# A two-layer trunk on one core: sums of weight blocks built in DRAM ahead of time, a seven-tile ring for weights, splits put forward

## The chip, the core and the metric

The kernel runs on one core of a Trainium2 chip, as one launch. The metric is the device time of that launch in microseconds (us): 1351.71 us is the median of 3 runs of the kernel before. Engines are named as in the profile: PE multiplies matrices, DVE and ACT work on tiles, POOL (GpSimd) does some tile work and issues transfers, SP issues transfers only.

## The reference, cut to what matters

The input is 512 positions of width 1024. Two layers follow, each a mixer (layer 0: gated delta net, layer 1: stick-breaking attention, both beside a small memory attention), an output projection, and an MLP of hidden width 4096. Only the lines that matter here:

```python
for i in range(DEPTH):                      # DEPTH = 2
    h = rms_norm(x, norm_pre_mix[i])
    proj = h @ (w_in_a if i == 0 else w_in_b)[0]
    ...
    x = x + rms_norm(y, norm_post_mix[i])
    h = rms_norm(x, norm_pre_mlp[i])
    y = jnp.square(jax.nn.relu(h @ w_up[i])) @ w_down[i]
    x = x + rms_norm(y, norm_post_mlp[i])
```

Everything is float32.

## The kernel before, in words

**Products.** A float32 product is done as three products of rounded parts: each operand is split into a high and a low part, and PE does high·high, high·low and low·high (`mm3`). A weight block of 512 KB (a piece) is loaded by SP into one of three tiles named `raw` (`raw`, L172). ACT copies it to the high part `whi` (L182) and DVE subtracts to get the low part `wlo` (L163); there are four places for such pairs. So a piece that is loaded early waits in `raw`, and the split waits for a free pair.

**Stages.** The span has, in order: the start and the memory keys (to about 50 us), the delta net of layer 0 (50 to 340), its output projection, the MLP of layer 0 (about 388 to 720), the attention of layer 1 (720 to 950), its output projection, the MLP of layer 1 (1005 to the end).

**The delta net.** `w_in_a` comes in 27 pieces, one for each call of `fm_slices`, which yields three times within a piece; `weave` puts the pieces' products between the steps of the recurrence. POOL does small work for the recurrence here, in its program order: masks (`dr_hi`, `dr_lo`, L382 and L383; `Dm`, L392), clears of `Q` (L489), and once for each group of heads the sum `vb` (L565), which PE transposes next (L368).

**The MLP.** The up product fills 32 chunks of hidden activations, 16, then 12, then 4. The down product of the 16 and of the 12 uses a scheme of seven products for each 2 by 2 block (`mlp_down`), with 4 and 3 blocks in the two groups, so 28 and 21 products in a layer. Its seven steps multiply combinations of the activations with combinations of four weight quarters B(0,0), B(0,1), B(1,0), B(1,1) of 512 KB each. `weave` puts the up pieces of the next group between them. The last 4 chunks go through `mlp_last` in the plain way.

**How the weight combinations are made before.** For each block, step 1 loads B(0,0) by SP into one of four tiles `xc` (`load`, L860). Steps 2, 3 and 7 add another quarter to that same tile by a transfer of POOL that accumulates (`plus`, L864). Step 4 loads B(0,0) again into `raw` and lets DVE subtract it from `xc` (`less`, L869). Steps 5 and 6 load a quarter plainly. In each step DVE also forms the activations' combination (`comb`, `minus`), ACT and DVE split it into `sh` (L902 and L163), and at the end of a step its result goes into `mixT` (L918).

**Order.** Each engine executes its own list in order. The list is the order of the code, changed by priorities: the scheduler may let an instruction that is ready go ahead of earlier code. `keep_in_program_order` ties an instruction to the one written before it on its engine and does not tie what comes after.

Of the kernel before, what the change touches and what calls it, by code (L numbers as in the profile page):

```python
# [8 lines left out]
F32 = mybir.dt.float32  # L9
# [4 lines left out]
ALU = mybir.AluOpType  # L14
# [15 lines left out]
MAGIC = float(0x5F3759DF)  # L30
NUA, NX, NSH = 15, 4, 4
NRAW = 3
NDM = 2
# [25 lines left out]
def drain(gen):  # L59
    for _ in gen:  # L60
        pass


class Trunk:
    def __init__(self, ctx, tc, a, out):
        self.ctx, self.tc, self.nc, self.a, self.out = ctx, tc, tc.nc, a, out
        pool = lambda **k: ctx.enter_context(tc.tile_pool(**k))
        self.const = pool(name="const", bufs=1)
        self.wp = pool(name="wp", bufs=1)
        self.act = pool(name="act", bufs=1)  # L70
        self.small = pool(name="small", bufs=3)
        self.ps = pool(name="ps", bufs=4, space=PSUM)
        self.decays = {}
        self.constants()
# [95 lines left out]
    def raw(self, src):  # L170
        raw = self.wp.tile(list(src.shape), F32, name="raw", tag="raw", bufs=NRAW)
        self.nc.sync.dma_start(out=raw, in_=src)  # L172
        return raw

    def halves(self, raw, alloc=None):
        shape = list(raw.shape)
        if alloc:
            hi, lo = alloc(F32R, shape), alloc(F32R, shape)
        else:
            hi = self.wp.tile(shape, F32R, name="whi", tag="whi", bufs=NW)  # L180
            lo = self.wp.tile(shape, F32R, name="wlo", tag="wlo", bufs=NW)
        self.nc.scalar.activation(out=hi, in_=raw, func=AF.Copy)  # L182
        self.split_lo(lo, raw, hi)
        return hi, lo
# [18 lines left out]
    def fm_slices(self, src, hi, lo, done, tag="acc"):  # L203
# [3 lines left out]
        for k0, k1 in ((0, 3), (3, 6), (6, 8)):  # L207
            self.fm_part(b, piece, hi, lo, k0, k1)
            if k1 == KC:
                done(b)  # L210
            yield (k1 - k0) * 3 * MM

# [621 lines left out]
    def mlp_up(self, i, c0, n, hi, lo, done):  # L834
# [4 lines left out]
        for c in range(c, c0 + n):  # L839
            yield from self.fm_slices(self.a["w_up"][i, c], hi, lo, done)  # L840

    def mlp_down(self, i, c0, nd, us, yacc, first, tail=None):

# [3 lines left out]
        nc, v = self.nc, self.nc.vector  # L847
        wd = self.a["w_down"][i]
        A, X = [], [None] * nd
        for d in range(nd):  # L850
# [3 lines left out]
        def B(d, kh, j):  # L854
            r0 = (c0 + 2 * (kh * nd + d)) * P
            return wd[r0:r0 + 2 * P, j * 512:(j + 1) * 512].rearrange("(z p) n -> p z n", p=P)

        def load(d):
            X[d] = self.ring("xc")
            nc.sync.dma_start(out=X[d], in_=B(d, 0, 0))  # L860
            return X[d]

        def plus(d, x, kh, j):
            nc.gpsimd.dma_start(out=x, in_=B(d, kh, j), accum_op=ALU.add)  # L864
            return x

        def less(d):
            x = self.raw(B(d, 0, 0))
            v.tensor_tensor(out=x, in0=X[d], in1=x, op=ALU.subtract)  # L869
            return x  # L870

# [4 lines left out]
        def minus(d):  # L876
# [4 lines left out]

        steps = (
            ("b", True, lambda d: A[d][11], lambda d: load(d), ((0, 0, 1),)),
            ("c", True, lambda d: comb(d, 21, 21, ALU.subtract, 22), lambda d: plus(d, X[d], 0, 1), ((1, 1, 1),)),
            ("b", False, lambda d: comb(d, 21, 21, ALU.subtract, 11), lambda d: plus(d, X[d], 1, 1), ((0, 1, -1),)),
            ("b", False, minus, lambda d: less(d), ((1, 1, -1),)),
            ("c", False, lambda d: comb(d, 21, 12, ALU.add, 21), lambda d: self.raw(B(d, 1, 1)), ((0, 1, 1),)),
            ("c", True, lambda d: A[d][12], lambda d: self.raw(B(d, 1, 0)), ((0, 0, 1),)),
            ("b", False, lambda d: A[d][22], lambda d: plus(d, X[d], 1, 0), ((1, 0, 1),)),
        )  # L890
        regions = {n: [self.bank("g") for _ in range(2)] for n in "bc"}
        fresh = {(r, j): first for r in range(2) for j in range(2)}
        for n, (name, new, left, right, outs) in enumerate(steps):
# [3 lines left out]
            for d in range(nd):  # L897
                w = right(d)
                whi, wlo = self.halves(w)
                src = left(d)  # L900
# [52 lines left out]

    def mlp(self, i, hi, lo, done):
        yacc = self.act.tile([P, NT, D], F32, name="mixT", bufs=1)
        groups = [{"n": 0, "t": []} for _ in GROUPS]
# [9 lines left out]
        for g, us in enumerate(groups):  # L966
# [5 lines left out]
            c += GROUPS[g]  # L972
        drain(tail)


# [126 lines left out]
def build(ctx, tc, a, out):  # L1102
# [14 lines left out]
    with tc.tile_pool(name="start", bufs=1) as sp:  # L1117
# [4 lines left out]
        for t in range(NT):  # L1122
# [3 lines left out]
            if t % 2:  # L1126
                k.to_T(t // 2, xs[t - 1:], k.g_pre[0], hi, lo)
        drain(kv)
    with tc.tile_pool(name="gdn", bufs=1, reuse_waits="tile") as gp:
        k.gdn_constants(gp)  # L1130
# [30 lines left out]
        for gi in range(3):  # L1161
            weave(k.gdn_group(gi, parts[gi], gp, mixT), fill(gi), SCALE[gi])
    keep = [dram.tile([P, D], F32, name=f"keep{t}") for t in range(NT)]

# [13 lines left out]
    with tc.tile_pool(name="mlp0", bufs=1, reuse_waits="tile") as k.mlpp:  # L1178
# [10 lines left out]
        k.mlp(0, hi, lo, done)  # L1189
        hi, lo = hi2, lo2  # L1190
    with tc.tile_pool(name="sb", bufs=1, reuse_waits="tile") as sp:
        tc.keep_in_program_order(nc.scalar.preload_act_table_set("natural_log_exp_and_others"))
# [39 lines left out]
    with tc.tile_pool(name="mlp1", bufs=1, reuse_waits="tile") as k.mlpp:  # L1232
# [6 lines left out]
        hi, lo = k.h_tiles()  # L1239
        k.out_proj(1, mixT, st, parked(1, k.next_norm(k.g_mlp[1], hi, lo)))  # L1240
        k.mlp(1, hi, lo, store)

# [55 lines left out]
```

## Time and profile before

| | |
|---|---|
| Median of 3 runs | 1351.71 us (1351.01 to 1354.47) |
| The profiled execution | 1353.73 us, of which the span is 1352.0 us |
| PE busy | 1290.3 us (95%) |
| DVE, ACT, POOL busy | 874.3, 723.8, 168.3 us |
| Mean busy share of the 16 transfer engines | queue of SP 26.5%, queue of POOL 12.9% |

A row of a time line reads: start, duration, engine, line, operation, out<-in, count, and in brackets the idle time before it and what ended that. A row of the windows gives the busy time of each engine in a stretch, its granted clock (PEclk, 1.00 is full), the mean busy share of the 16 transfer engines and GB/s.

### The profile page before, as it was taken

To read this page: it belongs to the slowest core of one execution; us is meant where nothing else is said; L and a number is where in the kernel's file an instruction comes from. 1 tells how busy PE (TensorE), PEld (TensorE's weight loads), DVE (VectorE), ACT (ScalarE), POOL (GpSimd) and SP (SyncE) were. 2 spreads that over 40 slices of the span, in tenths; PEclk is the share of its full clock that TensorE was granted. 3 is DMA by queue.
4 is the path that set the end of the run, shared out by engine and by line. 5 is a ranking of instruction groups with operands and counts; after the bars stand their busy time and mean duration, and the time that the engine had idled before them with its cause. 6 is when DMAs were issued, how large, how long until landed. Compare 5 with 4: busy or idle time off the path is not lost.

```text
span 1352.0 us, 18018 instructions
## 1 busy us (share of the span) xinstructions
PE 1290.3 (95%) x6620; PEld 1075.6 (80%) x6620; DVE 874.3 (65%) x1650; ACT 723.8 (54%) x1426; POOL 168.3 (12%) x194
## 2 busy tenths in 40 slices
PE   7999999998999999999989999988999999998987
PEld 6788888786798888887768987776798888887866
DVE  7677695876752366556678678889663356554866
ACT  8654535445554454454456577778555445444542
POOL 2511202000000111002000012223000021002100
PEclk9899999989999999999999999999999999999989
DMA  6421121112543465547644311110553365654732
GB/s 235 141 84 57 48 63 48 48 48 78 188 156 97 91 139 131 172 125 130 160 140 141 110 63 48 48 47 32 187 172 109 94 119 123 180 150 100 169 112 78
DMA packets 58409, 150.66 MB, mean 111 GB/s; under 512 B 4928, under 2 KB 10048, under 8 KB 58320
## 3 DMA queue, kind: packets, MB, share of 16 engines
q1 hardware_dynamic: 42256, 112.74, 26.5%
q0 software_dynamic: 15488, 35.72, 12.9%
q8 instruction: 52, 0.85, 0.3%
q10 hardware_dynamic: 576, 1.05, 0.2%
q14 instruction: 37, 0.30, 0.1%
HBM read 140.57 MB, written 8.91 MB: 111 GB/s over the span
## 4 chain that ended last, share of the span: by engine, by line
PE 58%; DVE 6%; ACT 4%; issue 2%; DMA 1%; POOL 0%; DVEq 0%; ACTq 0%; POOLq 0%
PE ps_acc L195 33%; PE ps_g L909 20%; PE ps_g L195 2%; PE ps_g L1057 1%; DMA raw<-w_down 1%; DVE wlo L163 1%; DMA xc<-w_down 1%; PE ps_g L277 1%; PE ps_acc L1074 1%; POOL sb_al L1063 0%; ACT scrap L263 0%; DVE ua L163 0%; ACT whi L182 0%; ACT sb_e L1038 0%; DVE sbkk L163 0%
## 5 line engine op out<-in xcount | busy, mean ns | idle before, releaser
L195 PE MATMUL ps_acc<-h_hi,wlo 128*128 128x512 f32 (+1 forms) x888 | 337.3, 380 | 3.7 <-DVE wlo L163 3.7
L195 PE MATMUL ps_acc<-h_hi,whi 128*128 128x512 f32 (+1 forms) x888 | 339.7, 382 | 1.2 <-DVE sbkk L163 1.2
L195 PE MATMUL ps_acc<-h_lo,whi 128*128 128x512 f32 (+1 forms) x888 | 336.0, 378 | 0.0
L163 DVE TENSOR_TENSOR wlo<-raw,whi 128x1024 fp32r<-128x1024 f32 x167 | 209.8, 1258 | 187.6 <-ACT whi L182 179.5
L182 ACT ACTIVATE whi<-raw 128x1024 fp32r<-128x1024 f32 x167 | 176.9, 1060 | 253.1 <-PE ps_acc L195 126.8
L909 PE MATMUL ps_g<-whi,sh 128*128 128x512 f32 x784 | 259.6, 396 | 3.6 <-DVE sh L163 2.5
L195 PEld LDWEIGHTS ps_acc<-h_hi,wlo 128*128 128x128 f32 x888 | 168.0, 189 | 34.8 <-DVE wlo L163 4.6
L195 PEld LDWEIGHTS ps_acc<-h_hi,whi 128*128 128x128 f32 x888 | 168.5, 190 | 29.7 <-DVE sbkk L163 1.5
L195 PEld LDWEIGHTS ps_acc<-h_lo,whi 128*128 128x128 f32 x888 | 168.5, 190 | 28.3
L909 PEld LDWEIGHTS ps_g<-whi,sh 128*128 128x128 f32 x784 | 147.3, 188 | 40.4 <-DVE sh L163 3.4
L909 PE MATMUL ps_g<-wlo,sh 128*128 128x512 f32 x392 | 155.2, 396 | 0.7 <-DVE wlo L163 0.7
L163 DVE TENSOR_TENSOR wlo<-xc,whi 128x1024 fp32r<-128x1024 f32 x56 | 67.9, 1222 | 68.5 <-ACT whi L182 67.9
L864 POOL DMA_DIRECT2D xc<-w_down x42 | 50.2, 1199 | 485.8 <-DVE wlo L163 409.8
L182 ACT ACTIVATE whi<-xc 128x1024 fp32r<-128x1024 f32 x56 | 59.0, 1057 | 96.2 <-PE ps_g L909 72.9
L909 PEld LDWEIGHTS ps_g<-wlo,sh 128*128 128x128 f32 x392 | 73.9, 189 | 18.7 <-DVE wlo L163 1.9
L163 DVE TENSOR_TENSOR sh<-ua,sh 128x512 fp32r<-128x512 f32 x98 | 66.8, 685 | 9.5 <-ACT sh L902 9.5
L195 PE MATMUL ps_acc<-ua 128*128 128x512 f32 x224 | 63.3, 415 | 8.0 <-ACT ua L182 7.4
L1063 POOL TENSOR_TENSOR sb_al<-sb_a,sb_ah 128x128 fp32r<-128x128 f32 (+3 forms) x48 | 46.7, 973 | 163.3 <-DVE sb_ah L1062 130.0
L902 ACT ACTIVATE sh<-ua 128x512 fp32r<-128x512 f32 x98 | 60.7, 619 | 10.7 <-DVE ua L163 10.4
L195 PEld LDWEIGHTS ps_acc<-ua 128*128 128x128 f32 x224 | 43.8, 200 | 20.1 <-ACT ua L182 8.3
L869 DVE TENSOR_TENSOR raw<-xc,raw 128x1024 f32<-128x1024 f32 x14 | 17.1, 1223 | 44.4 <-DMA raw<-w_down 27.1
L195 PE MATMUL ps_acc<-whi,h_hi 128*128 128x256 f32 (+1 forms) x144 | 44.6, 328 | 0.0
(351 smaller groups left out, 2154.0 us busy)
## 6 DMA issues: line engine op xcount, KB each, us to landing
raw<-w_up SPq DMA_DIRECT2D x64, 512.0 KB, 3.8
raw<-w_down SPq DMA_DIRECT2D x50, 512.0 KB, 4.4
xc<-w_down POOLq DMA_DIRECT2D x42, 512.0 KB, 6.4
raw<-w_in_a SPq DMA_DIRECT2D x27, 512.0 KB, 3.6
raw<-w_out SPq DMA_DIRECT2D x16, 512.0 KB, 3.6
xc<-w_down SPq DMA_DIRECT2D x14, 512.0 KB, 3.9
raw<-w_b_qk SPq DMA_DIRECT2D x14, 512.0 KB, 3.7
park<-xc POOLq DMA_DIRECT2D x8, 512.0 KB, 3.3
```

The lines of the kernel that those rows point to most:

```text
L163: self.nc.vector.tensor_tensor(out=lo, in0=src, in1=f(hi), op=ALU.subtract)
L182: self.nc.scalar.activation(out=hi, in_=raw, func=AF.Copy)
L195: self.nc.tensor.matmul(out, lhsT=l, rhs=r, start=start and k == 0 and i == 0, stop=stop and k == n - 1 and i == 2)
L277: nc.tensor.transpose(b[:, j, i * P:(i + 1) * P], xs[i][:, (kc + j) * P:(kc + j + 1) * P], self.ident)
L864: nc.gpsimd.dma_start(out=x, in_=B(d, kh, j), accum_op=ALU.add)
L869: v.tensor_tensor(out=x, in0=X[d], in1=x, op=ALU.subtract)
L902: nc.scalar.activation(out=s[:, 0], in_=src, func=AF.Copy)
L909: nc.tensor.matmul(y[t], lhsT=l, rhs=r, start=new and d == 0 and z == 0 and m == 0, stop=d == nd - 1 and z == 1 and m == 2, skip_group_che ...
L1057: nc.tensor.matmul(zb[:, off:n], lhsT=l, rhs=x, start=False, stop=m == len(ops) - 1, skip_group_check=True)
L1063: nc.gpsimd.tensor_tensor(out=u["al"], in0=a, in1=f(u["ah"]), op=ALU.subtract)
L1074: nc.tensor.matmul(ob[:, i * P:], lhsT=v, rhs=r, start=i == NT - 1 and m == 0, stop=i == 0 and m == 1, skip_group_check=True)
```

## The change

1. `prepare(i)` makes four DRAM tiles for each of the seven blocks of layer i: the sums 1 (B(0,0)+B(0,1)), 2 (sum 1 + B(1,1)), 3 (B(0,1) alone, then + B(1,1)) and 4 (sum 2 + B(1,0)), with the signs of the scheme left to the activations. It queues 56 operations: 28 copies from DRAM to DRAM on SP's queue and 28 accumulating transfers into DRAM on POOL's queue, in the waves copy 1, copy 3, plus 1, plus 3, copy 2, plus 2, copy 4, plus 4, seven of each. Each is tied to program order on its engine.
2. The queue is emptied from `fm_slices`, `rate` operations when a piece's last matmuls are written: 3 for each piece of the delta net (layer 0's sums), 1 for each piece in the MLP of layer 0, 2 in the attention of layer 1 (layer 1's sums).
3. In `mlp_down` the seven weight blocks are plain loads: three of quarters, four of sums. The 21 accumulations, 7 loads into `xc` and 7 DVE subtractions of a layer are gone.
4. Inside `mlp` the four `xc` tiles join the three `raw` tiles as one ring of seven (`wide`).
5. The splits of the weights in `mlp_down` get the priority of code 60 instructions earlier (`AHEAD`).

```diff
+AHEAD = 60
...
     def raw(self, src):
-        raw = self.wp.tile(list(src.shape), F32, name="raw", tag="raw", bufs=NRAW)
+        self.turn = (self.turn + 1) % (NRAW + NX)
+        if self.wide and self.turn >= NRAW:
+            raw = self.ring("xc", F32, src.shape)
+        else:
+            raw = self.wp.tile(list(src.shape), F32, name="raw", tag="raw", bufs=NRAW)
         self.nc.sync.dma_start(out=raw, in_=src)
         return raw
...
-    def halves(self, raw, alloc=None):
+    def halves(self, raw, alloc=None, ahead=0):
+        if ahead:
+            with self.tc.high_priority(offset=ahead):
+                return self.halves(raw, alloc)
...
             if k1 == KC:
                 done(b)
+                for _ in range(min(self.rate, len(self.background))):
+                    self.background.pop(0)()
...
+        def copy(dst, src):
+            self.tc.keep_in_program_order(nc.sync.dma_start(out=dst, in_=src))
+
+        def plus(dst, src):
+            self.tc.keep_in_program_order(nc.gpsimd.dma_start(out=dst, in_=src, accum_op=ALU.add))
...
+        waves = ((1, copy, (0, 1)), (3, copy, (0, 1)), (1, plus, (0, 0)), (3, plus, (1, 1)), (2, copy, 1), (2, plus, (1, 1)),
+                 (4, copy, 2), (4, plus, (1, 0)))
+        for n, op, src in waves:
+            for g, q in todo:
+                self.background.append(lambda g=g, q=q, n=n, op=op, src=src:
+                                       op(t[g, n], t[g, src] if isinstance(src, int) else q(*src)))
...
-            ("b", True, lambda d: A[d][11], lambda d: load(d), ((0, 0, 1),)),
-            ("c", True, lambda d: comb(d, 21, 21, ALU.subtract, 22), lambda d: plus(d, X[d], 0, 1), ((1, 1, 1),)),
-            ("b", False, lambda d: comb(d, 21, 21, ALU.subtract, 11), lambda d: plus(d, X[d], 1, 1), ((0, 1, -1),)),
-            ("b", False, minus, lambda d: less(d), ((1, 1, -1),)),
-            ("c", False, lambda d: comb(d, 21, 12, ALU.add, 21), lambda d: self.raw(B(d, 1, 1)), ((0, 1, 1),)),
-            ("c", True, lambda d: A[d][12], lambda d: self.raw(B(d, 1, 0)), ((0, 0, 1),)),
-            ("b", False, lambda d: A[d][22], lambda d: plus(d, X[d], 1, 0), ((1, 0, 1),)),
+            ("b", True, lambda d: A[d][11], lambda d: B(d, 0, 0), ((0, 0, 1),)),
+            ("c", True, lambda d: comb(d, 21, 21, ALU.subtract, 22), lambda d: T(d, 1), ((1, 1, 1),)),
+            ("b", False, lambda d: comb(d, 21, 21, ALU.subtract, 11), lambda d: T(d, 2), ((0, 1, -1),)),
+            ("b", False, minus, lambda d: T(d, 3), ((1, 1, -1),)),
+            ("c", False, lambda d: comb(d, 21, 12, ALU.add, 21), lambda d: B(d, 1, 1), ((0, 1, 1),)),
+            ("c", True, lambda d: A[d][12], lambda d: B(d, 1, 0), ((0, 0, 1),)),
+            ("b", False, lambda d: A[d][22], lambda d: T(d, 4), ((1, 0, 1),)),
...
-                whi, wlo = self.halves(w)
+                whi, wlo = self.halves(w, None, AHEAD)
...
     def mlp(self, i, hi, lo, done):
+        self.wide = True
...
+    k.prepare(0)
+    k.rate = 3
...
+    for op in k.background:
+        op()
+    k.background.clear()
+    k.prepare(1)
+    k.rate = 1
...
+    k.rate = 2
```

**The order on POOL around `vb`, in the delta net of layer 0.** Before, from the second `Dm` pair of the second group of heads to the clears behind `vb`:

```order
L392 TENSOR_TENSOR Dm<-dE,strictu 128x4x128
L392 TENSOR_TENSOR Dm<-dE,triu 128x4x128
L489 MEMSET Q 128x16x16 x2
L565 TENSOR_TENSOR vb<-vb,fo 128x512
L489 MEMSET Q 128x8x32 x2
```

Now, from the same `Dm` pair (L404 is the old L392, L501 the old L489, L577 the old L565; `sum_5_4` is sum 4 of block 5):

```order
L404 TENSOR_TENSOR Dm<-dE,triu 128x4x128
L874 DMA sum_3_2_613<-w_down 256x512
L874 DMA sum_4_2_617<-w_down 256x512
L874 DMA sum_5_2_621<-w_down 256x512
L874 DMA sum_6_2_625<-w_down 256x512
L394 TENSOR_TENSOR dr_hi<-triu,ghi 128x512
L395 TENSOR_TENSOR dr_lo<-triu,glo 128x512
L501 MEMSET Q 128x16x16 x2
L874 DMA sum_5_4_623<-w_down 256x512
L874 DMA sum_6_4_627<-w_down 256x512
L577 TENSOR_TENSOR vb<-vb,fo 128x512
L874 DMA sum_0_4_603<-w_down 256x512
```

Two accumulations into sum 4 stand ahead of `vb` now, and behind them wait the other five of that wave; the accumulations into the sums 1 and 3, 14 of them, stand between the fourth `Dm` of the delta net and the next clears of `Q`.

**The order on SP at the second and third waves of copies.** Before, the 27 pieces stand one after the other:

```order
L172 DMA raw<-w_mem_k 128x1024 x2
L172 DMA raw<-w_mem_kv 128x4x256 x2
L172 DMA raw<-w_in_a 128x1024 x27
L172 DMA raw<-w_out 128x1024 x7
L1170 DMA xc<-x 128x1024 x4
```

Now the 14 copies of the waves 1 and 3 stand between the first six pieces, and behind the 12th piece it reads:

```order
L871 DMA sum_5_2_621<-sum_5_1_620 16x8192
L871 DMA sum_6_2_625<-sum_6_1_624 16x8192
L179 DMA raw<-w_in_a 128x1024 x6
L871 DMA sum_0_4_603<-sum_0_2_601 16x8192
L871 DMA sum_1_4_607<-sum_1_2_605 16x8192
L871 DMA sum_2_4_611<-sum_2_2_609 16x8192
L871 DMA sum_3_4_615<-sum_3_2_613 16x8192
L179 DMA raw<-w_in_a 128x1024
L871 DMA sum_4_4_619<-sum_4_2_617 16x8192
L871 DMA sum_5_4_623<-sum_5_2_621 16x8192
L871 DMA sum_6_4_627<-sum_6_2_625 16x8192
L179 DMA raw<-w_in_a 128x1024 x8
```

The copy into sum 4 of block 6 reads sum 2 of that block, so it waits for the accumulation `sum_6_2`, and the accumulation `sum_6_4` on POOL waits for that copy.

**The order on PE at the end of the up product, layer 1.** Before, the last up piece (`h_hi`, `h_lo`) is followed by 25 products of the last four chunks (`ua`), and the down product's sixth step (`ps_g<-whi,sh`) comes after them:

```order
L195 MATMUL ps_acc_11678<-h_hi_9191,whi_11674 128x512
L195 MATMUL ps_acc_11678<-h_lo_9192,whi_11674 128x512
L195 MATMUL ps_acc_11678<-h_hi_9191,wlo_11675 128x512
L195 MATMUL ps_acc_11874<-ua_11787,ua_11394 128x512
L195 MATMUL ps_acc_11888<-ua_11787,ua_11394 128x512
L195 MATMUL ps_acc_11874<-ua_11788,ua_11394 128x512
L195 MATMUL ps_acc_11874<-ua_11787,ua_11394 128x512
```

Now 36 products of the down product's fifth step stand there, and 48 of `ua` follow in one piece:

```order
L205 MATMUL ps_acc_11871<-h_lo_9373,whi_11867 128x512
L205 MATMUL ps_acc_11871<-h_hi_9372,wlo_11868 128x512
L940 MATMUL ps_g_11485<-whi_12004,sh_12008 128x512
L940 MATMUL ps_g_11485<-wlo_12005,sh_12008 128x512
L940 MATMUL ps_g_11486<-whi_12004,sh_12008 128x512
L940 MATMUL ps_g_11486<-wlo_12005,sh_12008 128x512
L940 MATMUL ps_g_11485<-whi_12004,sh_12008 128x512
L940 MATMUL ps_g_11486<-whi_12004,sh_12008 128x512
```

The number of instructions on PE and on ACT is the same before and now; DVE has 14 fewer.

## Rows read from the trace of the kernel before

**Rows 1.** The page: busy times, and granted clock of PE in 40 slices.
```profile
PE 1290.3 (95%) x6620; PEld 1075.6 (80%) x6620; DVE 874.3 (65%) x1650; ACT 723.8 (54%) x1426; POOL 168.3 (12%) x194
...
PEclk9899999989999999999999999999999999999989
```

**Rows 2.** Window in the MLP of layer 1.
```profile
1085.00:1232.00 147.00, 147.00 (x637) 119.46 (x636) 84.05 (x93) 73.30 (x102) 14.00 (x12) 1.00 0.57 139
```

**Rows 3.** Time line of PE in the two MLPs, rows with idle time of over 1 us and what follows.
```profile
628.41 0.50 PE L195 MATMUL ps_acc<-h_hi,wlo 128*128 128x512 f32 x1 [1.49 <-DVE wlo L163]
...
632.48 0.96 PE L909 MATMUL ps_g<-whi,sh 128*128 128x512 f32 x3 [1.24 <-DVE sh L163]
...
683.81 0.73 PE L195 MATMUL ps_acc<-ua 128*128 128x512 f32 x2 [3.71 <-ACT ua L182]
685.07 7.22 PE L195 MATMUL ps_acc<-ua 128*128 128x512 f32 x23 [0.52 <-DVE ua L163]
...
1245.93 0.50 PE L195 MATMUL ps_acc<-h_hi,wlo 128*128 128x512 f32 x1 [2.24 <-DVE wlo L163]
...
1249.99 0.97 PE L909 MATMUL ps_g<-whi,sh 128*128 128x512 f32 x3 [1.25 <-DVE sh L163]
...
1301.18 8.73 PE L195 MATMUL ps_acc<-ua 128*128 128x512 f32 x25 [3.70 <-ACT ua L182]
```

**Rows 4.** The chain of waits, 1230 to 1252 us: start, us, what.
```profile
1234.78 8.30 DMA xc<-w_down
...
1245.87 1.19 DVE mixT L918 x2
1247.06 2.27 DVE wlo L163 x2
1249.34 0.61 DVE sh L163
```

**Rows 5.** The page: the two groups of instructions that the change removes.
```profile
L864 POOL DMA_DIRECT2D xc<-w_down x42 | 50.2, 1199 | 485.8 <-DVE wlo L163 409.8
...
L869 DVE TENSOR_TENSOR raw<-xc,raw 128x1024 f32<-128x1024 f32 x14 | 17.1, 1223 | 44.4 <-DMA raw<-w_down 27.1
```

**Rows 6.** Time line of POOL in the delta net.
```profile
69.47 2.27 POOL L392 TENSOR_TENSOR Dm<-dE,triu 128x512 f32<-128x512 f32 x1
...
138.94 1.27 POOL L392 TENSOR_TENSOR Dm<-dE,triu 128x512 f32<-128x512 f32 x1
...
167.17 1.48 POOL L565 TENSOR_TENSOR vb<-vb,fo 128x512 f32<-128x512 f32 x1 [23.03 <-DVE fo L563]
```

**Rows 7.** Time line of PE at the same place.
```profile
168.70 0.66 PE L368 MATMUL ps_g<-ident,vb 128*128 128x128 f32 x4 [0.24 <-POOL vb L565]
```

**Rows 8.** Time line of SP's queue, 25 to 210 us: the pieces of the delta net.
```profile
29.07 180.04 SPq L172 DMA_DIRECT2D raw<-w_in_a  x26
```

**Rows 9.** Queues in four stretches (60–300, 613–625, 481–491, 383–388.5): packets, MB, share of 16 engines.
```profile
q1 hardware_dynamic: 3744, 13.63, 18.7%
...
q0 software_dynamic: 800, 1.56, 77.5%
...
q0 software_dynamic: 544, 1.05, 63.8%
q1 hardware_dynamic: 144, 0.52, 13.4%
...
q0 software_dynamic: 144, 0.52, 23.3%
```

**Rows 10.** Transfers issued in 481–491 us and in 60–300 us: count, KB, us to landing.
```profile
raw<-w_up SPq DMA_DIRECT2D x1, 512.0 KB, 6.5
...
raw<-w_in_a SPq DMA_DIRECT2D x19, 512.0 KB, 3.6
```

**Rows 11.** Window of the first 122 us of layer 0's MLP.
```profile
388.00:510.00 122.00, 122.00 (x616) 103.88 (x615) 51.94 (x61) 59.54 (x87) 10.78 (x9) 1.00 0.45 104
```

**Rows 12.** Time line of POOL in the attention of layer 1, one of its gaps.
```profile
808.81 0.46 POOL L1063 TENSOR_TENSOR sb_al<-sb_a,sb_ah 128x128 fp32r<-128x128 f32 x1 [3.99 <-DVE sb_ah L1062]
```

More of the change, by code (lines that the diff above doesn't have):

```diff
@@ L66, in __init__ @@
         self.ctx, self.tc, self.nc, self.a, self.out = ctx, tc, tc.nc, a, out
+        self.background, self.rate, self.sums = [], 0, {}
+        self.turn, self.wide = 0, False
         pool = lambda **k: ctx.enter_context(tc.tile_pool(**k))
@@ L840, in mlp_up, with quarter, prepare @@
             yield from self.fm_slices(self.a["w_up"][i, c], hi, lo, done)
+    def quarter(self, i, c0, nd, d, kh, j):
+        r0 = (c0 + 2 * (kh * nd + d)) * P
+        return self.a["w_down"][i][r0:r0 + 2 * P, j * 512:(j + 1) * 512]
+    def prepare(self, i):
+        nc = self.nc
+        t = self.sums[i] = {}
+        c0, todo = 0, []
+        for n in GROUPS:
+            for d in range(n // 4):
+                todo.append((c0 // 4 + d, lambda kh, j, d=d, c0=c0, nd=n // 4: self.quarter(i, c0, nd, d, kh, j)))
+            c0 += n
+        def copy(dst, src):
[3 more added lines that the diff above has]
+        for g, q in todo:
+            for n in (1, 2, 3, 4):
+                t[g, n] = self.dram.tile([2 * P, 512], F32, name=f"sum{i}_{g}_{n}")
+        waves = ((1, copy, (0, 1)), (3, copy, (0, 1)), (1, plus, (0, 0)), (3, plus, (1, 1)), (2, copy, 1), (2, plus, (1, 1)),
+                 (4, copy, 2), (4, plus, (1, 0)))
+        for n, op, src in waves:
+            for g, q in todo:
+                self.background.append(lambda g=g, q=q, n=n, op=op, src=src:
+                                       op(t[g, n], t[g, src] if isinstance(src, int) else q(*src)))
     def mlp_down(self, i, c0, nd, us, yacc, first, tail=None):
         nc, v = self.nc, self.nc.vector
-        wd = self.a["w_down"][i]
-        A, X = [], [None] * nd
+        A = []
         for d in range(nd):
@@ L854, in B, with T @@
         def B(d, kh, j):
[L855 to L870, printed above, removed]
+            return self.raw(self.quarter(i, c0, nd, d, kh, j).rearrange("(z p) n -> p z n", p=P))
+        def T(d, n):
+            return self.raw(self.sums[i][c0 // 4 + d, n].rearrange("(z p) n -> p z n", p=P))
         def comb(d, o, a, op, b):
@@ L973, in mlp @@
         drain(tail)
+        self.wide = False
     def sb_values(self, hi, lo, pool, later):
@@ L1240, in build @@
         k.out_proj(1, mixT, st, parked(1, k.next_norm(k.g_mlp[1], hi, lo)))
+        for op in k.background:
+            op()
+        k.background.clear()
         k.mlp(1, hi, lo, store)
```

## The prediction

> **What bounds the kernel now.** I read the page first. PE is busy 95% of the span and its granted clock is near full in all slices [rows 1], so the time is PE's list of products plus what PE waits, plus what it does at the lower clock after a wait. The number of PE's instructions is the same before and after, so the change can only move waits. Next I took windows of the MLPs: in 1085 to 1232 us PE has no gap at all, although the transfer engines work 0.57 of the time and DVE and ACT about half [rows 2]; 388 to 510 us in layer 0 is as full [rows 11]. What the change saves on DVE and POOL in these stretches (per run 42 accumulations at 1.2 us of POOL and 14 subtractions at 1.2 us of DVE, [rows 5]) is hidden behind PE and worth nothing there by itself. Then PE's time line in the rest of the MLPs: there are six waits of over 1 us, at two places in each layer [rows 3]. The chain of waits says what the first place is [rows 4]: at 1234.78 an accumulation into `xc` takes 8.30 us, the subtraction waits for it in DVE's in-order list, and the splits queued behind the subtraction (`wlo`, `mixT`, `wlo`, `sh`) come late. The second place is the end of the up product, where PE has 25 products of `ua` next and their last split is not done.
>
> **The gain, in the MLPs.** Waits that I count: 1.49 + 1.24 + 3.71 = 6.4 us in layer 0, and 2.24 + 1.25 + 3.70 = 7.2 us in layer 1 [rows 3]. After the 3.7 us wait PE runs slowly for a while: 23 products take 7.22 us and 25 take 8.73 us [rows 3], where 637 in 147 us [rows 2] make 0.231 us each, so 23 and 25 should take 5.3 and 5.8 us; that loses 1.9 and 2.9 us. Together 13.6 + 4.8 = 18.4 us.
>
> What of it goes? With sums that lie finished in DRAM, no subtraction waits for an accumulation, and the weights of the next group can be loaded and split early, with seven tiles and the earlier priority. What stays at the first place is the chain of DVE behind the last product of a group: `mixT` twice (1.19), two `wlo` (2.27) and `sh` (0.61) [rows 4]. The `wlo` may go earlier; I keep 1.5 us per layer, near the 1.2 us that the `sh` wait has in both layers. At the second place 36 products of step 5 (36 × 0.231 = 8.3 us) now stand ahead of the `ua` products and cover the late split of 3.7 us; but step 5's own left operand is split behind the same relu on ACT, so I keep a third, 1.3 us per layer, too short for the clock to fall. Kept: 5.6 us. Gain: 18.4 − 5.6 = **13 us** (10 if twice as much stays at one place, 18 if all goes).
>
> **What it adds, and where that lies.** Four stretches get the 112 transfers.
>
> *MLP of layer 0*: 14 copies and 13 accumulations come in 388 to 510 us. The engines work 0.45 × 122 = 55 us there now [rows 11]; 8 old accumulations at 3.1 go. With the prices chosen below, 55 − 25 + 14 × 1.9 + 13 × 3.3 = 99 us of 122: it fits, and the seven-tile ring and four split places hold several pieces ahead. Nothing; at the high prices 129 of 122, some 7 us late.
>
> *Attention of layer 1*: 14 accumulations there take POOL 1.2 us each [rows 5], two at a time; POOL's gaps between its own steps, 4.0 us in the row shown [rows 12], hold a pair. Nothing; if a pair met each of seven pieces without cover it would be 7 × 2.4 = 17 us on POOL, but not all on PE.
>
> *MLP of layer 1*: plain loads in place of accumulations, fewer engine-microseconds. Nothing added.
>
> *Delta net of layer 0*: all 56 operations of layer 0. The order on POOL decides here. The 14 accumulations of the sums 1 and 3 stand behind the fourth `Dm`, which ends at 71.7 us [rows 6]. After them come seven into sum 2, then `sum_5_4` and `sum_6_4`, and only then `vb`. `sum_6_4` waits for its copy, that for `sum_6_2`, that for the whole wave ahead of it. Before, POOL is idle for 23 us ahead of `vb` [rows 6], but only because `vb`'s input comes at 167.17; PE already waits 0.24 us for `vb` [rows 7]. So the slack of `vb` is zero: each microsecond that POOL comes late there is one of PE, and behind `vb` on POOL stand the other accumulations and the next `Q`, behind the transpose on PE the rest of the list.
>
> **When does POOL reach `vb`?** The prices of one 512 KB transfer, in time of all 16 engines: a load into SBUF, 0.187 × 240 us / 26 = 1.73 us; when it stands behind other work, 0.134 × 10 = 1.34 us; an accumulation into SBUF, 0.775 × 12 / 3 = 3.1 us; a write from SBUF to DRAM, 0.233 × 5.5 = 1.28 us [rows 9]. No row shows a copy from DRAM to DRAM or an accumulation into DRAM. A copy costs at least a load that queues well (1.34) and at most a load and a write one after the other (1.73 + 1.28 = 3.0); I take 1.9, nearer to the load, since an engine that reads one block while it writes another is what the 1.34 shows. The accumulation costs at least 3.1 if the place of the result does not matter, at most 3.1 + 1.28 = 4.4; I take 3.3. Loads at 1.5.
>
> Do the two queues overlap? In 481 to 491 us two accumulations and one load take 0.638 + 0.134 = 0.77 of the engines, nearly all of the busy part, and the load needs 6.5 us to land where loads in the delta net need 3.6 [rows 9, 10]. So the work adds up. A rule of the Trainium skill speaks against this change, "DMA: Bandwidth & Descriptors", section "Issuing engines are not separate DMA queues": queues of several engines share the same 16 transfer engines, and spreading work over them saves issue time only. The trace agrees (0.77 as the sum of the two). By it the time is the forecast's, and rival A below is left with cheap transfers alone.
>
> From 29 us [rows 8] the first 14 copies and ten pieces (14 × 1.9 + 10 × 1.5 = 42 us) are through at about 71 us, just when POOL comes to its first accumulation. From 71.7 on: 21 accumulations × 3.3 = 69.3, 14 copies × 1.9 = 26.6, 9 pieces × 1.5 = 13.5, together 109.4 us: to 181.1. Add 2 us for the last to land beyond its share (3.6 − 1.73, [rows 9, 10]) and two issues of 1.2 us on POOL: 185.5, against 167.2. **`vb` comes 18 us late.** At the low ends (1.34, 3.1, 1.34) the sum is 95.9 us and `vb` 5 us late; at the high ends (3.0, 4.4, 1.73) it is 150 us, 17 us of the first copies are left at 71.7, and `vb` is 76 us late. After an idle time of over 3.7 us PE runs slowly, which cost 1.9 and 2.9 us above: 2.4 us once. Other POOL work, as the `Dm` at 138.94 [rows 6], stands behind up to 17 accumulations as well; those need only be issued, which is 17 × 1.2 = 20 us of the 67 us from 71.7 on.
>
> "Latency and other measured facts" of the same page gives 214 GB/s for copies within DRAM, which would be an estimate of 2.45 us for a copy; by it the sum would be 7.7 us more and `vb` 26 us late. No run here shows it.
>
> **The sum.** The profiled execution took 1353.7 us (span 1352.0 and 1.7 around it), 2.0 over the median of the runs. 1353.7 − 13 + 18.3 + 2.4 = 1361.4; less the 2.0: **1359 us**, 0.6% slower. A difference under 0.3% (4 us) is about what a measurement of this kernel cannot tell from none.
>
> **The rivals.**
>
> *A: the background work is in time.* If the queues overlap better than in the one window (accumulations leave the engines idle while they wait for their reads), only the dependences count: POOL issues the last accumulation into sum 2 behind the `Dm` at 138.94, so at about 146; it lands 6.5 us later and a copy takes 3.6, so POOL is at `vb` before 160, ahead of its input. For it: a load by itself takes 3.6 us to land and 1.73 us of the engines [rows 9, 10], so it leaves time that others could fill. Against: the 6.5 us load. Time 1351.7 − 13 = 1339 us (1334 to 1343), faster by 0.9%. Low prices do nearly the same. It decides at a sum of 98 us in place of 109: `vb` is then under 7 us late.
>
> *B: late by 7 to 14 us.* Prices between the low ends and mine: 1351.7 − 13 + 11 + 2.4 = 1352 us, no difference.
>
> *C: high prices.* Copies of 3.0 and accumulations of 4.4: `vb` 76 us late, and 7 us in the MLP: 1351.7 − 13 + 76 + 2.4 + 7 = 1424 us. For it: a result in DRAM is written and, for an accumulation, read there. Against: an accumulation into SBUF already pays for its second operand.
>
> *D: the MLP waits stay* since the left operand, not the weight, is what is late at the end of the up product: the gain is 6 in place of 13. It moves every case by 7 us; with `vb` late that is 1366 us.
>
> **How the numbers follow.** `vb` late by 14 to 35 us (with or without D): 0.40, own range 1353 to 1376. A: 0.30. B: 0.17. C and what lies between (35 to 76 us late): 0.13. The range that leaves out 2 in 10 goes from the middle of A to the low part of C: 1337 to 1383. Faster by over 0.3%: A and the low edge of B, 0.32. Within: the rest of B and the lower edge of the forecast, 0.18. Slower: 0.50.
>
> **What would show it.** PE's time line near 168 us: a wait of some 18 us ended by POOL's `vb`, and on POOL a gap ahead of `sum_5_4` or `sum_6_4` that a copy ends; then some 5 us at a lower clock. The queue rows in 72 to 185 us: engines nearly always busy, POOL's queue the larger; prices from them (copies 1.9, accumulations 3.3). In the MLPs: no wait of 3.7 us ahead of `ua`, no `xc` accumulation in the chain, and PE idle under 3 us in each. The prediction is wrong if PE passes 168 us without a wait, if a wait comes at another instruction of POOL (`Q` or `Dm`) or at a piece, or if the MLPs keep their waits.

## The result, and the profile after

The change takes 1359.06 us (median of 5 runs, 1358.19 to 1360.75), 1.0053 times the kernel before, interval [1.0039, 1.0068]. The forecast was 1359 us, slower. The number is met, and both halves of its sum are nearly met too, but the loss came mostly at other places than the working said.

The time line of PE in the profiled execution after, its rows with idle time that answer to [rows 3] and [rows 7]:

```profile
53.47 1.11 PE L308 MATMUL ps_g<-ident,ba_sb 128*128 128x128 f32 x4 [6.51 <-ACT ba_sb L305]
104.24 1.09 PE L380 MATMUL ps_g<-ident,kb 128*128 128x128 f32 x4 [6.27 <-DVE kb L434]
110.60 5.16 PE L452 MATMUL ps_g<-kq,kT 128*128 128x256 f32 x12 [3.14 <-ACT kq L444]
...
188.43 1.11 PE L380 MATMUL ps_g<-ident,vb 128*128 128x128 f32 x4 [5.19 <-POOL vb L577]
...
356.65 0.65 PE L380 MATMUL ps_g<-ident,vb 128*128 128x128 f32 x4 [2.23 <-DVE vb L577]
...
698.69 0.50 PE L940 MATMUL ps_g<-whi,sh 128*128 128x512 f32 x1 [1.21 <-ACT sh L933]
727.42 0.69 PE L289 MATMUL ps_g<-ident,mixT 128*128 128x128 f32 x2 [3.58 <-DVE rstd_a L263]
843.52 0.44 PE L1107 MATMUL ps_acc<-sb_al,v 128*128 128x384 f32 x1 [0.71 <-POOL sb_al L1096]
...
1312.13 0.50 PE L940 MATMUL ps_g<-whi,sh 128*128 128x512 f32 x1 [1.21 <-ACT sh L933]
```

The same instructions of the kernel before, for the shift between the two:

```profile
336.12 0.66 PE L368 MATMUL ps_g<-ident,vb 128*128 128x128 f32 x4 [2.24 <-DVE vb L565]
...
826.55 0.44 PE L1074 MATMUL ps_acc<-sb_al,v 128*128 128x384 f32 x1 [0.70 <-POOL sb_al L1063]
```

Read the shifts first. The first `vb` transposes start at 188.43, where [rows 7] has 168.70: 19.7 us late. The last `vb` is 20.5 us late (356.65 against 336.12). In the attention of layer 1 it is 17.0 (843.52 against 826.55), and at the end 7.1 (spans of 1359.1 and 1352.0). So the delta net loses 20.5 us, the MLP of layer 0 gives back 3.5 and that of layer 1 9.9: 13.4 together. The working had 18.3 + 2.4 = 20.7 and 13.

Then read what ends the waits. `vb` accounts for some 5 us of the loss (5.19 less the 0.24 of before). At 53 us PE waits 6.5 (before 2.55 at a neighbouring instruction), at 104 us 6.3, at 111 us 3.1. The chain of waits after, 28 to 200 us, names the cause:

```profile
39.10 12.69 DMA raw<-w_in_a
...
76.61 9.22 DMA sum<-w_down
85.84 0.48 SPq L871
86.42 8.57 DMA raw<-w_in_a
...
99.94 8.50 DMA raw<-w_in_a
...
156.59 24.99 DMA sum<-w_down
181.60 4.31 DMA sum<-sum
```

A piece of `w_in_a` that took 3.6 us to land [rows 10] takes 12.7 us at 39, behind nine copies on the same queue. Those copies wait for nothing: here it is their work, ahead of the piece, that makes it late. At 76 to 109 us the link is another: an accumulation (9.2 us) has to land, SP then issues its copy, and only then the piece. SP's own time line shows the pieces between the copies:

```profile
83.29 3.03 SPq L871 DMA_DIRECT2D sum<-sum  x2
86.42 0.52 SPq L179 DMA_DIRECT2D raw<-w_in_a  x1
90.00 9.84 SPq L871 DMA_DIRECT2D sum<-sum  x3
99.94 0.53 SPq L179 DMA_DIRECT2D raw<-w_in_a  x1
```

and ACT waits for those two pieces:

```profile
95.08 1.06 ACT L192 ACTIVATE whi<-raw 128x1024 fp32r<-128x1024 f32 x1 [4.28 <-DMA raw<-w_in_a]
108.52 1.06 ACT L192 ACTIVATE whi<-raw 128x1024 fp32r<-128x1024 f32 x1 [8.23 <-DMA raw<-w_in_a]
```

POOL's time line has the order that the prediction spoke of (`sum_5_4` and `sum_6_4` at 183.48 and 186.42, `vb` behind them), and a gap that it did not:

```profile
103.56 0.88 POOL L874 DMA_DIRECT2D sum<-w_down  x1 [3.04 <-DMA sum<-w_down]
138.75 0.31 POOL L501 MEMSET Q<- 128x256 f32 x1 [34.32 <-PE ps_g L517]
...
150.22 0.31 POOL L501 MEMSET Q<- 128x256 f32 x1 [0.58 <-PE ps_g L517]
150.72 2.71 POOL L874 DMA_DIRECT2D sum<-w_down  x3 [0.18 <-issue]
...
183.48 0.88 POOL L874 DMA_DIRECT2D sum<-w_down  x1 [21.37 <-DMA sum<-sum]
186.42 0.89 POOL L874 DMA_DIRECT2D sum<-w_down  x1 [2.06 <-DMA sum<-sum]
187.01 1.36 POOL L577 TENSOR_TENSOR vb<-vb,fo 128x512 f32<-128x512 f32 x1
```

For 34 us POOL waits for PE, with the wave into sum 2 queued behind that wait and the clears that follow it. The last of these clears starts at 150.22, and the wave right behind it. In the kernel before, the same clear starts at 135.43:

```profile
135.43 0.31 POOL L489 MEMSET Q<- 128x256 f32 x1 [0.22 <-PE ps_g L505]
```

SP's queue in 28 to 75 us and POOL's in 76 to 110 us give the prices, in packets, MB and share of the 16 engines:

```profile
q1 hardware_dynamic: 5138, 12.08, 76.2%
...
q0 software_dynamic: 2094, 4.06, 68.6%
```

In the first stretch 12.08 MB are 23 blocks of 0.524 MB (14 copies, the rest pieces) in 0.762 × 47 = 35.8 us: 1.56 us each, where I had 1.9 and 1.5. (That is a mean of both kinds; with 1.73 or 1.34 us for a piece, as in [rows 9], it leaves 1.45 or 1.70 for a copy.) In the second, 4.06 MB are 7.7 accumulations into DRAM in 0.686 × 34 = 23.3 us: 3.0 us each, where I had 3.3. Windows after show the transfer engines and the clock:

```profile
104.00:112.00 8.00, 4.62 (x14) 3.63 (x15) 3.25 (x6) 2.51 (x4) 0.44 (x1) 0.50 1.01 247
...
118.00:150.00 32.00, 31.50 (x193) 27.09 (x191) 23.43 (x66) 13.92 (x28) 6.45 (x7) 1.00 0.62 152
150.00:182.00 32.00, 32.00 (x194) 27.55 (x194) 19.56 (x51) 16.56 (x47) 11.71 (x14) 1.00 0.98 231
...
727.00:745.00 18.00, 17.58 (x74) 14.41 (x75) 14.16 (x31) 8.09 (x19) 0.54 (x1) 0.83 0.43 146
```

The engines are full to 118 us, at 0.62 to 150, full again to 182: they are not busy throughout. After the waits the granted clock is at the lower of its levels (0.50 in 104 to 112).

In the MLPs, all four waits at the start of the second group are gone; at the end of the up product 1.21 us stays in each layer; and layer 0 has a new one of 3.58 us, at the transposes for the next stage, with a clock of 0.83 behind it.

### The profile page after: what moved, and what is told of

The parts are those of the page before. It is cut to its first block, busy times and chain, and to the rows that moved or that the text cites. A ratio compares the mean times of both kernels' runs of the same rounds, so it can differ in the third digit from the quotient of the medians.

```text
span 1359.1 us, 18225 instructions
## 1 busy us (share of the span) xinstructions
PE 1289.3 (95%) x6620; PEld 1079.1 (79%) x6620; DVE 857.4 (63%) x1636; ACT 723.1 (53%) x1426; POOL 167.0 (12%) x208
## 3 DMA queue, kind: packets, MB, share of 16 engines
q10 hardware_dynamic: 576, 1.05, 0.2%
## 4 chain that ended last, share of the span: by engine, by line
PE 73%; DVE 10%; ACT 7%; DMA 6%; issue 2%; POOL 1%; DVEq 0%; SPq 0%; ACTq 0%; POOLq 0%
PE ps_acc L205 40%; PE ps_g L940 19%; PE ps_g L205 4%; DMA sum<-w_down 3%; DMA raw<-w_in_a 2%; PE ps_g L1090 1%; PE ps_g L380 1%; DVE wlo L166 1%; PE ps_g L509 1%; ACT scrap L275 1%; ACT whi L192 1%; PE ps_g L517 1%; PE ps_g L479 1%; PE ps_g L452 1%; DMA raw<-sum 1%
## 5 line engine op out<-in xcount | busy, mean ns | idle before, releaser
L166 DVE TENSOR_TENSOR wlo<-raw,whi 128x1024 fp32r<-128x1024 f32 x130 | 162.8, 1254 | 159.6 <-ACT whi L192 154.2
L192 ACT ACTIVATE whi<-raw 128x1024 fp32r<-128x1024 f32 x130 | 137.4, 1058 | 226.1 <-PE ps_acc L205 95.2
L166 DVE TENSOR_TENSOR wlo<-xc,whi 128x1024 fp32r<-128x1024 f32 x93 | 113.7, 1225 | 158.3 <-ACT whi L192 150.8
L192 ACT ACTIVATE whi<-xc 128x1024 fp32r<-128x1024 f32 x93 | 98.6, 1060 | 146.2 <-PE ps_g L940 101.5
L874 POOL DMA_DIRECT2D sum<-w_down x56 | 52.1, 1402 | 97.4 <-DMA sum<-w_down 61.3
L205 PE MATMUL ps_acc<-ua 128*128 128x512 f32 x224 | 57.6, 392 | 0.0
```

Of the source, the lines that this page charges most:

```text
L166: self.nc.vector.tensor_tensor(out=lo, in0=src, in1=f(hi), op=ALU.subtract)
L205: self.nc.tensor.matmul(out, lhsT=l, rhs=r, start=start and k == 0 and i == 0, stop=stop and k == n - 1 and i == 2)
L874: self.tc.keep_in_program_order(nc.gpsimd.dma_start(out=dst, in_=src, accum_op=ALU.add))
```

## The experiments

Two theories of the loss in the delta net. **S** is the prediction's: POOL reaches `vb` when the work of the transfer engines is through, and that is the loss. **H**, formed on the trace above: the loss comes from waiting transfers in SP's in-order list, with pieces behind them; `vb` is its smaller part. **M** asks whether layer 1's sums cost something too.

**1. No sums at all.** `T` loads a quarter, `prepare` is not called.

```diff
         def T(d, n):
-            return self.raw(self.sums[i][c0 // 4 + d, n].rearrange("(z p) n -> p z n", p=P))
+            return B(d, 0, 1)
...
-    k.prepare(0)
-    k.rate = 3
...
-    k.prepare(1)
-    k.rate = 1
```

> The change without any transfer that makes sums: neither layer has copies or accumulations in DRAM, and where a sum was loaded a plain quarter of the weights is loaded (this part of the computation is left out). The ring of seven tiles and the earlier splits stay. Theory S (the prediction's: the sums of layer 0 are made while the delta net runs, and POOL comes to vb only when all that work is through) and theory H (pieces stand on SP's queue behind copies; vb is only the smaller part) both give 1359.1 less the 20 us by which PE is behind at 357 us: 1338 to 1340 us, no wait at vb, none at a piece. Theory M (the transfers of layer 1's sums cost time in the MLP of layer 0 and in the attention as well): under 1336 us.

1336.7 us, ratio to the kernel before 0.9894 [0.9870, 0.9918]. The gain without the making of sums is 14 us, the forecast's 13. The time lies between the two forecasts, and the interval, some 3 us to each side, covers both, so M is left to run 2. In the trace PE has no wait of over 1 us from 55 to 289 us, so none at `vb` and none at a piece.

**2. No sums of layer 0.**

```diff
         def T(d, n):
+            if i == 0:
+                return B(d, 0, 1)
             return self.raw(self.sums[i][c0 // 4 + d, n].rearrange("(z p) n -> p z n", p=P))
...
-    k.prepare(0)
-    k.rate = 3
```

> The change without the sums of layer 0 (plain quarters are loaded in their place, this part of the computation is left out); those of layer 1 are made as before in the MLP of layer 0 and in the attention. Theories S and H: as the run without any sums, within 1.5 us, so 1338 to 1341 us. Theory M: longer than that run by 3 us or more, with new waits between 390 and 950 us.

1337.3 us, 0.9897 [0.9882, 0.9911]: the same as without any. Layer 1's 56 transfers, in the MLP of layer 0 and in the attention, cost nothing that can be measured. The two intervals alone could hide 3 us, but the traces don't: the same products of PE come 3.1 us later than in run 1 at 344 us, when the first of layer 1's transfers is issued (345 us), and 2.7 at 950 us, and between 390 and 950 us PE has no wait of over 0.8 us that run 1 has not. M falls, and the whole loss lies with layer 0's.

**3. The two waves into sum 4 held back, so that `vb` is free.**

```diff
     k.prepare(0)
+    held, k.background = k.background[42:], k.background[:42]
     k.rate = 3
...
         for gi in range(3):
             weave(k.gdn_group(gi, parts[gi], gp, mixT), fill(gi), SCALE[gi])
+        k.background += held
+        held = []
```

> The change with the last two waves of layer 0 (copy 4, plus 4) put forward only after the first two groups' code, so that nothing of them stands ahead of vb on POOL; all else is as in the change. Theory S: vb was the place where the work of the transfer engines came to the path, so nearly all of the 20 us go: 1339 to 1342 us. Theory H: the waits for pieces at about 53, 104 and 111 us stay (6.5, 6.3 and 3.1 us and the lower clock behind them), only the 5.2 us at vb and some 2 us of lower clock go: 1350 to 1353 us.

1365.0 us, 1.0104 [1.0086, 1.0121]: neither number. The edit holds the transfers back further than the expectation says, until behind the code of all three groups: the seven copies are issued at 308 us, the seven accumulations at 354. The time line of PE, rows with idle time:

```profile
53.31 1.11 PE L308 MATMUL ps_g<-ident,ba_sb 128*128 128x128 f32 x4 [6.42 <-ACT ba_sb L305]
106.52 1.09 PE L380 MATMUL ps_g<-ident,kb 128*128 128x128 f32 x4 [8.99 <-DVE kb L434]
114.48 4.58 PE L452 MATMUL ps_g<-kq,kT 128*128 128x256 f32 x12 [4.74 <-ACT kq L444]
...
186.78 0.66 PE L380 MATMUL ps_g<-ident,vb 128*128 128x128 f32 x4 [0.24 <-POOL vb L577]
...
397.69 2.18 PE L289 MATMUL ps_g<-ident,ua 128*128 128x128 f32 x9 [6.10 <-DVE ua L278]
416.62 1.53 PE L289 MATMUL ps_g<-ident,ua 128*128 128x128 f32 x12 [3.37 <-DVE ua L278]
```

`vb` waits 0.24 us as before the change, and is 18.1 us late all the same (186.78 against 168.70 in [rows 7]). S would have it on time, so S falls as the main cause. The total is up because the seven held accumulations, which land until 389 us, now meet the transfers of the output projection: a transfer from `xc` to DRAM that is issued at 380 us needs 11.1 us to land, where it needs 2.9 in the change, a load waits for its tile, and PE waits 6.1 and 3.4 us behind. Here it is the work of the transfers that costs. The earlier waits (at 53, 107 and 114 us) are also some 4 us longer in sum than in the change, and why is not shown.

**4. The copies into sum 2 by POOL.**

```diff
-        def copy(dst, src):
-            self.tc.keep_in_program_order(nc.sync.dma_start(out=dst, in_=src))
+        def copy(dst, src, eng=nc.sync):
+            self.tc.keep_in_program_order(eng.dma_start(out=dst, in_=src))
+
+        def copy_pool(dst, src):
+            copy(dst, src, nc.gpsimd)
...
-        waves = (... (2, copy, 1), (2, plus, (1, 1)),
+        waves = (... (2, copy if i else copy_pool, 1), (2, plus, (1, 1)),
```

> The change with the seven copies of layer 0's wave 2 (sum 1 to sum 2), which wait for accumulations, issued by POOL in place of SP, ahead of the clears of Q; same transfers, same sizes. Theory S: the work is the same, so POOL is at vb at about 187 us again; the waits at the pieces go and the one at vb grows to some 17 us: 1357 to 1360 us. Theory H: the pieces behind these copies come in time, the waits of 6.3 and 3.1 us and the lower clock behind them go, and vb waits some 5 us as now: 1346 to 1349 us.

1349.7 us, 0.9988 [0.9975, 1.0002]: 0.7 us above H's range and 7 under S's, so on H's side. PE, rows with idle time:

```profile
100.76 0.63 PE L380 MATMUL ps_g<-ident,kb 128*128 128x128 f32 x4 [1.76 <-DVE kb L434]
182.00 1.12 PE L380 MATMUL ps_g<-ident,vb 128*128 128x128 f32 x4 [9.26 <-POOL vb L577]
```

With the same transfers, the two waits of 6.3 and 3.1 us become one of 1.8. `vb` is then due earlier, and its wait grows to 9.3 us; H had 5. So a part of S holds: once the pieces are on time, the chain of accumulations does end at `vb`, where PE waits 9 us and not 17 or 18.

**5. A pause ahead of the copies into sum 2.** Eighteen empty turns (`None`, for which no transfer is issued), six pieces.

```diff
-    k.rate = 3
+    bg = k.background
+    k.background = bg[:28] + [None] * 18 + bg[28:]
+    k.rate = 3
```

> The change with a pause of six pieces of the delta net between wave 4 of layer 0's sums (plus 3) and the copies into sum 2: the copies then stand on SP behind pieces whose turn comes when the accumulations have long landed, and no accumulation into sum 4 stands ahead of the first vb. The number and size of the transfers are those of the change. Theory H (what costs is the place of waiting transfers in two in-order lists, not the work): only the wait of 6.5 us at 53 us stays, which is 4 us more than the kernel before has there, so the run without any sums plus 4: 1339 to 1343 us. Theory S (work of the transfer engines): the same 56 transfers still collide with the pieces, 1348 to 1356 us.

1339.1 us, 0.9914 [0.9891, 0.9936]. PE waits 6.10 us at 52 and 2.75 at 100, and has no wait of over 0.6 us from there to 297 us:

```profile
52.43 1.11 PE L310 MATMUL ps_g<-ident,ba_sb 128*128 128x128 f32 x4 [6.10 <-ACT ba_sb L307]
100.10 0.63 PE L382 MATMUL ps_g<-ident,kb 128*128 128x128 f32 x4 [2.75 <-DVE kb L436]
...
297.74 2.10 PE L519 MATMUL ps_g<-X,Q 128*128 128x64 f32 x16 [1.82 <-DVE Q L512]
```

All 112 transfers of the change are made, only later in two lists, and 20 of the change's 1359 us are gone.

One rival is left: that the pieces at 86 and 100 us are late only since the transfer engines are full, and that a pause helps by spreading the work. The traces settle it. These are the pieces that SP issues in 76 to 110 us, with the median time from issue to landing, in the change, in run 4 and in run 5:

```profile
raw<-w_in_a SPq DMA_DIRECT2D x2, 512.0 KB, 8.5
...
raw<-w_in_a SPq DMA_DIRECT2D x6, 512.0 KB, 7.2
...
raw<-w_in_a SPq DMA_DIRECT2D x5, 512.0 KB, 7.2
```

and the window in the change and in run 5:

```profile
76.00:110.00 34.00, 25.19 (x116) 20.44 (x114) 19.67 (x37) 12.27 (x31) 12.58 (x15) 0.88 1.05 257
...
76.00:110.00 34.00, 31.25 (x148) 25.69 (x147) 25.64 (x48) 16.02 (x46) 12.87 (x15) 0.95 1.06 235
```

The engines are equally full (1.05, in run 4 1.04, in run 5 1.06; a transfer counts whole in the window where it starts, so a share can pass 1), and a piece needs 7 to 8.5 us to land in all three. What differs is when SP issues them: the eleventh to thirteenth piece at 86.4, 99.9 and 110.7 us in the change, at 77.9, 83.0 and 88.2 in run 5. Where no copy holds these pieces back, PE waits 1.8 us here in run 4 and 2.8 in run 5 (H had none); in the change it waits 9.4. That is H for the larger part. The wait at 53 us is not H's, since the copies there wait for nothing.

**6. The pause, and a slow start.** The first seven copies come one for each piece; the 14 empty turns among them and four behind make the same 18.

```diff
-    k.background = bg[:28] + [None] * 18 + bg[28:]
+    k.background = [x for op in bg[:7] for x in (op, None, None)] + bg[7:28] + [None] * 4 + bg[28:]
```

> As the run with the pause, and the first seven copies come one for each piece in place of three, so that the fourth to sixth piece no longer stand behind nine to fourteen copies. Theory H: the wait at 53 us falls from 6.5 to the 2.6 us of the kernel before, and nothing of the delta net's sums is left to see: as the run without any sums, 1336 to 1339 us. If the accumulations that come later for it wait ahead of vb: 1342 to 1348 us, with a wait ended by vb.

1337.1 us, 0.9894 [0.9872, 0.9916]: the ratio of the run without any sums, with all sums made. PE waits 1.68 us at 49 and 3.03 at 55, more than the 2.6 that I expected, and none of its waits of over 0.6 us up to 290 us is ended by `vb`. Against run 5 the intervals overlap.

**7. No earlier splits.** `AHEAD = 0`, on run 1.

> The run without any sums (plain quarters are loaded, so the sums are left out), and the splits without their earlier priority. The order of PE's list at the end of the up product is the same with it and without it. If the earlier splits remove the waits at the start of the second group (1.5 + 1.2 and 2.2 + 1.3 us in the kernel before): 3 to 6 us over the run without any sums, 1340 to 1343 us. If the plain loads and the seven tiles do that: 1336 to 1338 us, no difference.

1335.0 us, 0.9875 [0.9850, 0.9900], no longer than run 1. The earlier priority gives nothing that can be measured here.

**8. No ring of seven.** `self.wide = False`, on run 1.

> The run without any sums (plain quarters are loaded, so the sums are left out), and the MLP's loads through three raw tiles, not seven. The order of PE's list at the end of the up product is then that of the kernel before, with 25 products of ua ahead of the sixth step. If the wait of 3.7 us and the lower clock behind it come from that order: they return in both layers (5.6 and 6.6 us), less the waits that go (1.2 us in each layer, 2.7 us and its clock ahead of the transposes in layer 0): 2 to 5 us over the run without any sums, 1339 to 1342 us. If three tiles also starve PE between: over 1345 us.

1346.6 us, 0.9972 [0.9956, 0.9987], which is 0.0078 over run 1, some 10 us and more than expected. It is also the time of the rival, that three tiles starve PE, but apart from the three waits shown PE has none of over 0.65 us in the two MLPs. PE:

```profile
676.35 0.73 PE L205 MATMUL ps_acc<-ua 128*128 128x512 f32 x2 [3.71 <-ACT ua L192]
...
711.58 0.61 PE L289 MATMUL ps_g<-ident,mixT 128*128 128x128 f32 x2 [3.53 <-DVE rstd_a L263]
...
1292.85 8.96 PE L205 MATMUL ps_acc<-ua 128*128 128x512 f32 x25 [3.71 <-ACT ua L192]
```

The waits of 3.7 us and the slow products behind them are back (25 in 8.96 us), as the order on PE has again 25 `ua` products ahead of the sixth step. So the ring, by the order that it lets the scheduler find, removes the second place of [rows 3]. The waits at the first place stay away without the ring, as they do in run 7 without the earlier splits. So beside the plain loads either of the two is enough, or neither is needed; no run leaves out both. The wait ahead of the transposes does not go, against my expectation; that is the excess (5.6 + 6.6 − 2.4 + 0.8 = 10.6 us, where 0.8 is 3.53 less the 2.71 of run 1).

**9 and 10. The transposes later.** On run 6, offset −60 and −100.

```diff
+            elif t % 2 and later is not None:
+                with self.tc.high_priority(offset=-60):
+                    turn()
             elif t % 2:
                 turn()
```

> The run with the pause and the slow start, and the transposes of the next stage at the end of layer 0's MLP get the priority of code 60 instructions later: on PE all 36 products of the seventh step and 12 of ua now stand ahead of the first transpose, in place of 24 products. Theory T (the wait of 2.1 to 3.6 us there and the lower clock behind it are owed to that order, which came with the ring of seven tiles): the wait goes and some 2 us of lower clock with it, 1332 to 1335 us. Rival: the norm is late by itself and the wait moves to the next transposes: 1336 to 1339 us.

> As the run with 60, with 100: 26 products of ua stand ahead of the first transpose. Theory T: as with 60, within 1.5 us, 1332 to 1336 us; if the transposes come so late that the products of the next stage wait for them: a wait at the first product of the attention, 1336 us or more.

With 60: 1337.1 us, 0.9892 [0.9875, 0.9910], no gain. With 100: 1333.1 us, 0.9863 [0.9842, 0.9884]. The row at the transposes, with 60 and then with 100:

```profile
714.70 2.17 PE L291 MATMUL ps_g<-ident,mixT 128*128 128x128 f32 x14 [2.85 <-DVE mixT L280]
```

```profile
713.28 0.33 PE L291 MATMUL ps_g<-ident,mixT 128*128 128x128 f32 x1 [1.35 <-DVE mixT L280]
```

With 60 the wait only moved to the second half's transposes, as the rival had it. With 100 it is 1.35 us, where run 6 has 2.11. The wait is not owed to the ring, as theory T has it: run 8, without the ring, has it too. Run 10 is the fastest version with all of the reference's computation, 1.4% under the kernel before; against run 6 its interval overlaps, so the last 0.3% is not shown by the times. In the traces the stretch from 690 to 760 us, where the order was changed, is 2.5 us shorter than in run 6 (with 60 it is 0.1 shorter).

## Why the prediction was right, and where not

*The gain of 13 us in the MLPs*: right in sum (13.4 in the change, 14 in run 1). Its parts differ. At the start of the second group I kept 1.5 us per layer; nothing stays. At the end of the up product I kept 1.3; 1.21 stays, and the words on the left operand behind the relu are what the row says (`sh`, from ACT). The new wait of 3.58 us and its clock at layer 0's transposes was not in the sum. It about cancels what I had kept too much, so that layer 0 gives 3.5 us where the sum had 5.5, and layer 1 9.9 where it had 7.3.

*The cost nowhere else*: right. Run 2 shows that layer 1's sums are free in both stages.

*`vb` 18 us late*: the lateness is right (19.7), the way to it is wrong, at two steps. The first is a wait that I put at nothing without a reason: I named `vb`'s zero slack on POOL, and asked for no piece what stands ahead of it on SP, though the order showed copies that wait for accumulations between pieces. By these waits and the lower clock behind them PE is 14.8 us late well before `vb`. The second is the sum of work, which took the transfer engines as busy from 71.7 to 185 us. They stand at 0.62 in 118 to 150, since on POOL the wave into sum 2 stands behind clears of `Q` that PE releases. Even in the kernel before the last of those comes at 135.4 us; now PE is late, and it comes at 150.2. From there the accumulations into sum 2 and the copies into sum 4 keep the engines full until POOL comes to `vb` at 187, and that is the 5 us at `vb`.

My prices were too high by some 0.3 us each (1.9 against 1.56, 3.3 against 3.0); with the measured ones the sum gives 21 × 3.0 + 14 × 1.56 + 9 × 1.5 = 98 us, `vb` at 174, 7 us late, and a time of 1348 us. Too high prices stood in for the missing waits. In the estimate with 2.45 us for a copy the first 14 copies, too, would have ended later, at 78 us; it should have had `vb` some 33 us late, not 26.

The parts as measured: 4.0 + 6.0 + 3.1 us of waits at pieces (6.51 − 2.55, 6.27 − 0.31, where 0.31 is what the kernel before waits there, and 3.14), 5.0 at `vb`, and some 2.4 us net for the rest; I had put 2.4 for it, as one event at a lower clock. It is several. The same products stand 1.8 us later than before at 64 us, 14.8 from 116 to 182, 22.1 from 200 to 308 and 20.5 from 316 on. So the waits at 104 and 111 us cost 13 us together with the slow products around them, the wait at `vb` 7, and 1.5 us come back at 310 us, where the change runs at a higher clock than the kernel before did (0.79 in 314 to 322 against 0.57 in 292 to 300).

*The condition that I set*, "wrong if a wait comes at a piece", was met. Of the signs, the wait of some 18 us at `vb` did not come (5.2), nor did engines that are busy throughout, and in layer 0's MLP PE is idle for 4.8 us (1.21 + 3.58) and not under 3. That the time was right is luck: two errors, prices too high and waits left out, that cancel.

*Rivals*: A's number (1339 us) is what runs 5 and 6 reach, by another order and not by overlap. C's prices did not come, and the gain of 13.4 us rules out D.

## What to carry to other kernels

Background transfers cost here mostly by where they wait: a transfer that waits for another queue's result holds all that stands behind it in its issuer's list (20 of 1359 us, run 5). Their work costs too where it lies among loads that are due at once, as at 53 us and in the output projection of run 3. Before forecasting such a change, go through each issuing list and ask for each load what stands ahead of it and for what that waits; then give waiting transfers a pause so long that their inputs have landed by their turn. A sum of engine time is at best a lower bound for when a chain ends, so look in each list for what breaks the chain. A matching total doesn't show that its terms are right.

## What the runs showed of the hardware

A copy of 512 KB within DRAM costs the 16 engines about as much as a load into SBUF: 1.56 us as a mean over copies and pieces, where the kernel before has 1.73 for loads by themselves and 1.34 behind other work [rows 9]. In 157 to 182 us, where nearly all of SP's transfers are copies from one sum to another, 3.67 MB take 0.366 of 25 us: 1.31 us for each 512 KB. An accumulation into DRAM, 3.0 us, costs no more than one into SBUF, 3.1. I had expected both to pay for the write. The Trainium skill's figure in "DMA: Bandwidth & Descriptors", section "Latency and other measured facts", 214 GB/s, would have made a copy an estimated 2.45 us; the measurement here is well under that, for blocks and rows of another shape.
